# Two transformer blocks in one program: attention banks per head pair, paired expert products, and six buffers for one weight stream

## The chip, the cores and the metric

The kernel runs on one core of one Trainium2 chip. The metric is the time of one execution on the device, in microseconds (us); below 2167.4 us the kernel has become faster. The engines are TensorE (PE for its matmuls, PEld for its weight loads), VectorE (DVE), ScalarE (ACT), GpSimd (POOL) and SyncE (SP), which issues nearly all transfers. All arithmetic is on float32 values.

## The reference, cut to what matters

The program computes two blocks on 256 tokens of width 1024. The first block has two layers: each is a mixer, a SwiGLU network and a gated embedding. The mixer of layer 0, here "the even mixer", is the attention that the change touches:

```python
zb, zc, zh, q, k, v, qi, ki, wi = split_cols(h @ w_in, EVEN_SPLITS)
y_a = zb * causal_dwconv(zc * zh, conv_w)
q = apply_rope(rmsnorm(heads(q), q_norm_g), cos_a, sin_a)   # 8 heads of 64
k = apply_rope(rmsnorm(heads(k), k_norm_g), cos_a, sin_a)
qi, ki = partial_rope(qi, ...), partial_rope(layernorm(ki, ...), ...)
y_b = dsa_attention(q, k, v, qi, ki, wi)   # top-k keys chosen by qi, ki, wi
return concat([y_a, y_b]) @ w_out
```

Layer 1's mixer ("the odd mixer") is a gated delta rule with chunks of 64 tokens. The second block has two layers on the tokens and, in layer 0, on 256 context tokens too. Each takes its shifts, scales and gates from one vector, then mixes, then runs 16 experts, each of which picks 32 tokens of each stream:

```python
sh1, sc1, g1, sh2, sc2, g2 = split(silu(c) @ ada_w[i] + ada_b[i], 6)    # the "ada" product
...
a = einsum('becd,edf->becf', xs, w_gate);  u = einsum('becd,edf->becf', xs, w_up)
y = einsum('becf,efd->becd', silu(a) * u, w_down)                       # 16 experts of 1024 x 1024
```

## The kernel before, in words

The stages stand one behind another in the profile, in us from the span's start: even mixer 0 to 172, its network 172 to 362, embedding and odd mixer 362 to 660, network 660 to 860, embedding and the second block's first mixer (mix2 of layer 0) 860 to 1124, first expert stage 1124 to 1586, mix2 of layer 1 to 1736, second expert stage to the end.

In the dense stages a weight tile is loaded by SP, split into a high and a low part (line 174 on ACT, line 175 on DVE) and multiplied three times: lines 205 to 207 give features by tokens (lines 236 to 238 tokens by features). The code is written against a tile framework: every tile has a pool with a number of buffers, the framework adds the waits, and a scheduler with costs of its own sets the order of each engine's instructions. Each engine then runs its queue strictly in that order, so an instruction that waits holds all behind it. PSUM has eight banks: four of tag "a", three of "b", one of "f" (line 337).

In the even mixer line 485 transposes rotated queries and keys, line 538 makes the index scores. The attention goes over two blocks of 128 queries (tb) and four pairs of heads (hp). Line 601 is the product of queries and keys, lines 605 to 614 the softmax on DVE and ACT, line 617 transposes the probabilities, line 619 copies them, line 621 multiplies them with the values. The PSUM bank of line 621's result is held over all four pairs. Products that do not depend on it (lines 236 to 238 of the convolution branch) are ordered between.

The ada product is a generator (line 1082 on): 96 steps, each one load of 512 KB (line 1096) and four matmuls (line 1111); sixteen steps end in an addition (line 1116) and four transposes (line 1119). The stages before draw on it for steps to fill with, at a priority that lets the scheduler put them where PE would wait. Its tile "adaw" has `nbuf` = 3 buffers.

In the first expert stage both streams of 32 tokens share the stationary side, so 64 columns of PE are used by a gate product (line 1670, PSUM partitions 0 to 63) and the other 64 by an up product (line 1671, partitions 64 to 127). Per expert there are 16 of each, one SiLU and one product of 64x512 for each half n (lines 1681, 1682), transposes of that result (line 1691, eight of 64 rows), a copy (line 1693), 16 down products (line 1702), and every fourth expert gathers the tokens of the next four (line 1631) and scatters the results of four (line 1722). Its weights come as 12 tiles of 1 MB, issued by SP in the order in which the code asks for them (line 1593), into a ring of 24 buffers. An issue waits until its buffer is free and until the transfer eight issues earlier has landed.

## Time and profile before

| | us |
|---|---|
| median of three runs | 2167.4 (2166.94 to 2171.16) |
| profiled execution, its own time | 2173.54 |
| span of the profile | 2171.8 |
| first expert stage | 1124 to 1586 |
| even mixer | 0 to 172 |

The profile is that of one execution. Times of the rows are in us from the start of the span. A 512-column matmul of the expert stages stands in the trace as two records, as do the others on float32 values; a row "x4" is four records without another line between them. The number in brackets is idle time of the engine before the row, and behind the arrow is what ended it. The granted clock (PEclk) is the share of TensorE's full 2.4 GHz.

### The profile page before, as it was taken

How to read it: one execution, taken by the hardware profiler on the slowest of the kernel's cores; microseconds unless marked ns; L12 is line 12 of the kernel's file. 1: busy time of each engine (PE TensorE's matmuls, PEld its weight loads, DVE VectorE, ACT ScalarE, POOL GpSimd, SP SyncE). 2: the span in 40 equal slices, each digit the busy share in tenths (PEclk: the TensorE clock that was granted, in tenths of full speed). 3: DMA queues.
4: the chain of work that ended last, by engine and by line, in shares of the span. 5: the costliest groups of instructions: out<-in, count | busy, mean ns of one | idle time of the engine just before them, and what ended most of it. 6: DMA issues, size and time to landing. Idle time of an engine off the chain costs nothing.

```text
span 2171.8 us, 30574 instructions
## 1 busy us (share of the span) xinstructions
PE 1964.3 (90%) x12300; PEld 1240.6 (57%) x12300; DVE 930.0 (43%) x1969; ACT 669.8 (31%) x1310; POOL 84.2 (4%) x95
## 2 busy tenths in 40 slices
PE   7999999898989999999989999999989788777776
PEld 5687888677867888677753434343357523121211
DVE  7765555785655555754442221322166611010101
ACT  5454444663534444745320000000055300000000
POOL 0100000122010000210000000000000000000000
PEclk9999999999999999999989999999999899998998
DMA  6646676843347676731559999999964699999998
GB/s 237 218 138 232 218 233 199 268 146 108 128 135 233 221 240 205 249 122 57 205 230 415 420 420 420 420 420 418 379 240 175 252 407 420 421 420 420 420 421 341
DMA packets 209086, 611.83 MB, mean 282 GB/s; under 512 B 14736, under 2 KB 117424, under 8 KB 159792
## 3 DMA queue, kind: packets, MB, share of 16 engines
q1 hardware_dynamic: 202320, 603.08, 72.9%
q10 hardware_dynamic: 6624, 6.79, 1.1%
q8 instruction: 97, 1.59, 0.3%
q14 instruction: 45, 0.37, 0.0%
HBM read 608.78 MB, written 1.05 MB: 281 GB/s over the span
## 4 chain that ended last, share of the span: by engine, by line
PE 68%; DMA 20%; DVE 7%; issue 2%; ACT 2%; POOL 1%; SPq 0%; DVEq 0%; ACTq 0%; POOLq 0%
DMA w<-in_w_up_dram 11%; PE ps_a L1671 7%; DMA w<-in_w_down_dram 6%; PE ps_a L206 6%; PE ps_a L205 6%; PE ps_a L207 6%; PE ps_b L1702 5%; PE ps_a L1670 4%; PE ps_b L238 4%; PE ps_b L236 4%; PE ps_b L237 4%; PE ps_f L1111 2%; PE ps_b L1631 2%; DMA adaw<-in_ada_w_dram 2%; DVE wl L175 1%
## 5 line engine op out<-in xcount | busy, mean ns | idle before, releaser
L175 DVE TENSOR_TENSOR wl<-w,wh 128x512 fp32r<-128x512 f32 x540 | 369.7, 694 | 278.1 <-ACT wh L174 275.8
L174 ACT CAST wh<-w 128x512 fp32r<-128x512 f32 x540 | 331.1, 620 | 362.3 <-PE ps_a L207 164.7
L1670 PE MATMUL ps_a<-w,XS 128*64 128x512 f32 x512 | 233.2, 599 | 0.0
L1671 PE MATMUL ps_a<-w,XS 128*64 128x512 f32 x512 | 228.0, 595 | 0.0
L236 PE MATMUL ps_b<-xTh,wh 128*128 128x256 f32 x704 | 200.8, 285 | 0.5 <-ACT wh L174 0.5
L238 PE MATMUL ps_b<-xTh,wl 128*128 128x256 f32 x704 | 199.7, 284 | 1.7 <-DVE wl L175 1.7
L237 PE MATMUL ps_b<-xTl,wh 128*128 128x256 f32 x704 | 198.6, 282 | 0.0
L1742 PE MATMUL ps_b<-w,XS 128*32 128x512 f32 x1024 | 159.2, 633 | 43.5 <-DMA w<-in_w_up_dram 33.4
L236 PEld LDWEIGHTS ps_b<-xTh,wh 128*128 128x128 f32 x704 | 133.1, 189 | 10.0 <-ACT wh L174 8.4
L238 PEld LDWEIGHTS ps_b<-xTh,wl 128*128 128x128 f32 x704 | 134.8, 192 | 6.2 <-DVE wl L175 3.1
L1702 PE MATMUL ps_b<-w,hTe 128*64 128x512 f32 x512 | 138.4, 595 | 0.0
L237 PEld LDWEIGHTS ps_b<-xTl,wh 128*128 128x128 f32 x704 | 133.8, 190 | 2.2 <-issue 1.6
L205 PE MATMUL ps_a<-wh,xTh 128*128 128x512 f32 (+1 forms) x336 | 128.4, 386 | 3.7 <-ACT wh L174 1.9
L206 PE MATMUL ps_a<-wl,xTh 128*128 128x512 f32 (+1 forms) x336 | 129.9, 387 | 0.8 <-DVE wl L175 0.7
L207 PE MATMUL ps_a<-wh,xTl 128*128 128x512 f32 (+1 forms) x336 | 128.9, 384 | 0.0
L1742 PEld LDWEIGHTS ps_b<-w,XS 128*32 128x32 f32 x1024 | 35.6, 112 | 161.8 <-issue 68.8
L1671 PEld LDWEIGHTS ps_a<-w,XS 128*64 128x64 f32 x512 | 67.2, 137 | 102.0 <-issue 100.4
L1744 ACT ACTIVATE sge<-ps_b 64x512 f32<-64x512 f32 x16 | 9.5, 591 | 368.1 <-PE ps_b L1742 368.1
L1681 ACT ACTIVATE sge<-ps_a 64x512 f32<-64x512 f32 x32 | 18.9, 590 | 296.4 <-PE ps_a L1671 253.3
L1756 PE MATMUL ps_b<-w,hTe 128*32 128x512 f32 x512 | 91.2, 724 | 19.8 <-DMA w<-in_w_down_dram 11.5
L1745 DVE TENSOR_TENSOR sge<-sge,ps_b 64x512 f32<-64x512 f32 x16 | 11.0, 690 | 201.1 <-ACT sge L1744 201.1
L1709 DVE TENSOR_TENSOR Y<-ps_b,G 32x512 f32<-32x512 f32 x64 | 44.0, 687 | 104.0 <-PE ps_b L1702 102.8
(534 smaller groups left out, 3231.8 us busy)
## 6 DMA issues: line engine op xcount, KB each, us to landing
w<-in_w_gate_dram SPq DMA_DIRECT2D x128, 1024.0 KB, 19.9
w<-in_w_up_dram SPq DMA_DIRECT2D x128, 1024.0 KB, 19.8
w<-in_w_down_dram SPq DMA_DIRECT2D x128, 1024.0 KB, 19.8
adaw<-in_ada_w_dram SPq DMA_DIRECT2D x96, 512.0 KB, 6.0
w<-in_ffn_w_gate_dram SPq DMA_DIRECT2D x22, 1024.0 KB, 5.2
w<-in_ffn_w_up_dram SPq DMA_DIRECT2D x22, 1024.0 KB, 5.3
w<-in_ffn_w_down_dram SPq DMA_DIRECT2D x22, 1024.0 KB, 5.0
w<-in_od_w_in_dram SPq DMA_DIRECT2D x16, 1024.0 KB, 5.2
```

The lines of the kernel that those rows point to most:

```text
L174: nc.scalar.copy(h, raw)
L175: nc.vector.tensor_tensor(l, raw, h.bitcast(F32), op=ALU.subtract)
L205: mm(out, ah, bh, start=start, stop=False)
L206: mm(out, ah, bl, start=False, stop=False)
L207: mm(out, al, bh, start=False, stop=stop)
L236: mm(o, h[:, s], xT[0][:, k], start=(k == 0 and b % 2 == 0), stop=False, skip_group_check=True)
L237: mm(o, h[:, s], xT[1][:, k], start=False, stop=False, skip_group_check=True)
L238: self.last = mm(o, l[:, s], xT[0][:, k], start=False, stop=(k == nk - 1), skip_group_check=True)
L1670: mm(pg[n][0:64], XS[k][:, e % 4], wt[f"g{k // 2}"][:, k % 2, c], start=(k == 0), stop=(k == 7))
L1671: mm(pg[n][64:128], XS[k][:, e % 4], wt[f"u{k // 2}"][:, k % 2, c], start=(k == 0), stop=(k == 7))
L1702: mm(py[64 * n:64 * n + 64], hv[:, k], wt[f"d{k // 2}"][:, k % 2, n * 512:n * 512 + 512], start=(k == 0), stop=(k == 7))
L1742: mm(pg[32 * q:32 * q + 32], XS[k][:, ex], w[:, k % 2, c], start=(k == 0), stop=(k == 7))
```

## The change

In the even mixer the three projections go to SBUF by a copy as soon as they are complete (k, then v, then q), so their PSUM banks come free; v is projected before q. The index key's transposes are issued behind those of the index queries. Both heads of a pair share one bank for the transposed probabilities and one copy, and line 621's result gets a bank for each pair, which is split to SBUF pair by pair. Several SBUF tiles get more buffers. In the ada product `nbuf` goes from 3 to 6. In the first expert stage the up product is issued first and the gate product directly behind it; the eight transposes of 64 rows become four of 128; the down products take the halves in another order and their tiles are loaded as d0, d2, d1, d3. Three of the next expert's 16 gate and up pairs are now written ahead of the transposes, one behind them.

```diff
-            to_T(ki2, kiT, 1)
-            qi = at.tile([128, 2, 512], F32, tag="tokm", name="qi", bufs=2)
+            qi = at.tile([128, 2, 512], F32, tag="tokm", name="qi", bufs=3)
...
             to_T(qi, qiT, 4)
+            to_T(ki2, kiT, 1)
...
+            def project(c0, name):
+                acc = self.gemm_tok(xT, W, c0, 512)
+                t = at.tile([128, 2, 512], F32, tag="v" if name == "v" else "pj", name=name, bufs=1 if name == "v" else 2)
                 for tb in range(2):
+                    nc.scalar.copy(t[:, tb], acc[tb])
+                return t
...
-            ak = self.gemm_tok(xT, W, 2048, 512)
+            ak = project(2048, "ak")
             norm_rope(1, kT, ak)
-            aq = self.gemm_tok(xT, W, 1536, 512)
+            v = project(2560, "v")
+            aq = project(1536, "aq")
             norm_rope(0, qT, aq)
...
-                        pt = self.ps("b")
+                        if j == 0:
+                            pt = self.ps("b")
                         for kb in range(tb + 1):
-                            nc.tensor.transpose(pt[:, kb * 128:(kb + 1) * 128], pr[:, kb * 128:(kb + 1) * 128], ident)
-                        pT = at.tile([128, 256], F32, tag="pT", name="pT", bufs=2)
-                        nc.scalar.copy(pT[:, :nk], pt[:, :nk])
+                            nc.tensor.transpose(pt[:, j * 256 + kb * 128:j * 256 + (kb + 1) * 128],
+                                                pr[:, kb * 128:(kb + 1) * 128], ident)
+                    nc.scalar.copy(pT[:, :, :nk], pt.rearrange("p (j k) -> p j k", j=2)[:, :, :nk])
+                    po = self.ps("b")
+                    for j in range(2):
+                        h = 2 * hp + j
                         for kb in range(tb + 1):
-                            nc.tensor.matmul(po[64 * j:64 * j + 64, hp * 128:(hp + 1) * 128],
-                                             v[:, kb, h * 64:(h + 1) * 64], pT[:, kb * 128:(kb + 1) * 128],
-                                             start=(kb == 0), stop=(kb == tb))
-                pv = po.rearrange("p (h q) -> p h q", q=128)
-                self.split_to(yT[0][:, 4:8, ts], yT[1][:, 4:8, ts], pv)
+                            nc.tensor.matmul(po[64 * j:64 * j + 64, :128], v[:, kb, h * 64:(h + 1) * 64],
+                                             pT[:, j, kb * 128:(kb + 1) * 128], start=(kb == 0), stop=(kb == tb))
+                    self.split_to(yT[0][:, 4 + hp, ts], yT[1][:, 4 + hp, ts], po[:, :128])
...
-        nbuf = 3
+        nbuf = 6
...
-                        for n in range(2):
-                            c = slice(n * 512, n * 512 + 512)
+                        c = slice(n * 512, n * 512 + 512)
+                        up = mm(pg[n][64:128], XS[k][:, e % 4], wt[f"u{k // 2}"][:, k % 2, c], start=(k == 0), stop=(k == 7))
+                        with self.tc.issue_after(up.ins):
                             mm(pg[n][0:64], XS[k][:, e % 4], wt[f"g{k // 2}"][:, k % 2, c], start=(k == 0), stop=(k == 7))
-                            mm(pg[n][64:128], XS[k][:, e % 4], wt[f"u{k // 2}"][:, k % 2, c], start=(k == 0), stop=(k == 7))
...
-                        gate_up(e + 1, (0,))
+                        gate_up(e + 1, kn[:3])
...
-                    for n in range(2):
-                        for j in range(4):
-                            k = 4 * n + j
-                            nc.tensor.transpose(pt[:, k * 64:(k + 1) * 64], sg[64 * n:64 * n + 64, pair(j)],
-                                                self.ident[64 * n:64 * n + 64, 64 * n:64 * n + 64])
-                        V.tensor_copy(hT[:, n * 256:(n + 1) * 256], pt[:, n * 256:(n + 1) * 256])
+                    for j in range(4):
+                        nc.tensor.transpose(pt[:, j * 128:(j + 1) * 128], sg[:, pair(j)], self.ident)
+                    for j in range(0, 512, 256):
+                        V.tensor_copy(hT[:, j:j + 256], pt[:, j:j + 256])
...
-                    loads(e, [f"d{j}" for j in range(4)])
+                    loads(e, [f"d{j}" for j in (0, 2, 1, 3)])
```

How this moves PE's queue stands in three places. The first is the attention of the even mixer, a pair of heads of the second query block. Before (names as in the lines above: pr are probabilities, kT and qT keys and queries, xTh, wh and wl the convolution branch):

```order
L617 MATMUL ps_b_1109<-const_i_66,pr_1103 128x128 x2
L238 MATMUL ps_a_1386<-xTh_107,wl_1439 128x256
L236 MATMUL ps_a_1387<-xTh_107,wh_1438 128x256
L237 MATMUL ps_a_1387<-xTl_108,wh_1438 128x256
L238 MATMUL ps_a_1387<-xTh_107,wl_1439 128x256
L236 MATMUL ps_a_1387<-xTh_107,wh_1438 128x256
L621 MATMUL ps_b_1094<-pT_1112,v_864 64x128 x2
L617 MATMUL ps_b_1126<-const_i_66,pr_1120 128x128 x2
L601 MATMUL ps_b_1133<-kT_597,qT_596 128x256
L237 MATMUL ps_a_1387<-xTl_108,wh_1438 128x256
L621 MATMUL ps_b_1094<-pT_1129,v_864 64x128 x2
L601 MATMUL ps_b_1134<-kT_597,qT_596 128x256
```

In the changed kernel:

```order
L619 MATMUL ps_b_1108<-const_i_66,pr_1115 128x128 x2
L236 MATMUL ps_a_1542<-xTh_107,wh_1643 128x256
L237 MATMUL ps_a_1542<-xTl_108,wh_1643 128x256
L238 MATMUL ps_a_1542<-xTh_107,wl_1644 128x256
L236 MATMUL ps_a_1542<-xTh_107,wh_1643 128x256
L237 MATMUL ps_a_1542<-xTl_108,wh_1643 128x256
L238 MATMUL ps_a_1542<-xTh_107,wl_1644 128x256
L626 MATMUL ps_b_1124<-pT_1097,v_818 64x128 x4
L602 MATMUL ps_b_1131<-kT_597,qT_596 128x256
L602 MATMUL ps_b_1132<-kT_597,qT_596 128x256
```

Both heads' products with the values (now line 626) stand together, and behind them both of the next pair's products of keys and queries (now line 602).

The second place is PE in mix2 of layer 0, behind the start of its first norm (line 1178, now 1181). Before:

```order
L1111 MATMUL ps_f<-adaw,adastat 32x256 x5
L1178 MATMUL ps_b<-const_i,xn 128x128 x4
L1111 MATMUL ps_f<-adaw,adastat 32x256 x4
L205 MATMUL ps_a<-wh,xTh 128x512
L206 MATMUL ps_a<-wl,xTh 128x512
L1111 MATMUL ps_f<-adaw,adastat 32x256 x3
L207 MATMUL ps_a<-wh,xTl 128x512
L1178 MATMUL ps_b<-const_i,xn 128x128 x4
```

In the changed kernel:

```order
L207 MATMUL ps_a<-wh,xTl 128x512
L1181 MATMUL ps_b<-const_i,xn 128x128 x12
L205 MATMUL ps_a<-wh,xTh 128x512
L206 MATMUL ps_a<-wl,xTh 128x512
L207 MATMUL ps_a<-wh,xTl 128x512
L205 MATMUL ps_a<-wh,xTh 128x512
L1181 MATMUL ps_b<-const_i,xn 128x128 x4
L206 MATMUL ps_a<-wl,xTh 128x512
```

The ada matmuls (line 1111, now 1114) have gone from this stage. 384 of them stand in the program, two records each. At the norm that opens the odd mixer 164 of them stand behind PE before and 192 now; at the norm that follows that mixer 225 and 257; in the changed kernel all 384 stand ahead of the end of the network that ends at 860 us, where before 64 (16 steps) stand behind it.

The third place is PE at the boundary between two experts (sge is the SiLU product that is transposed; ps_a_12685 is the old expert's bank and ps_a_12860 and 12861 the next one's; in the changed kernel 12653, and 12824 and 12825). Before:

```order
L1670 MATMUL ps_a_12685<-w_12815,XS_12683 64x512
L1671 MATMUL ps_a_12685<-w_12817,XS_12683 64x512
L1691 MATMUL ps_b_12871<-const_i_66,sge_12855 128x64 x4
L1670 MATMUL ps_a_12860<-w_12862,XS_12676 64x512
L1670 MATMUL ps_a_12861<-w_12862,XS_12676 64x512
L1691 MATMUL ps_b_12871<-const_i_66,sge_12855 128x64 x4
L1671 MATMUL ps_a_12860<-w_12864,XS_12676 64x512
L1671 MATMUL ps_a_12861<-w_12864,XS_12676 64x512
L1670 MATMUL ps_a_12860<-w_12862,XS_12677 64x512
L1671 MATMUL ps_a_12860<-w_12864,XS_12677 64x512
L1670 MATMUL ps_a_12861<-w_12862,XS_12677 64x512
L1671 MATMUL ps_a_12861<-w_12864,XS_12677 64x512
```

In the changed kernel:

```order
L1674 MATMUL ps_a_12653<-w_12781,XS_12651 64x512
L1676 MATMUL ps_a_12653<-w_12779,XS_12651 64x512
L1695 MATMUL ps_b_12837<-const_i_66,sge_12819 128x128 x4
L1674 MATMUL ps_a_12824<-w_12828,XS_12644 64x512
L1676 MATMUL ps_a_12824<-w_12826,XS_12644 64x512
L1674 MATMUL ps_a_12825<-w_12828,XS_12644 64x512
L1676 MATMUL ps_a_12825<-w_12826,XS_12644 64x512
L1674 MATMUL ps_a_12824<-w_12828,XS_12645 64x512
L1676 MATMUL ps_a_12824<-w_12826,XS_12645 64x512
L1674 MATMUL ps_a_12825<-w_12828,XS_12645 64x512
L1676 MATMUL ps_a_12825<-w_12826,XS_12645 64x512
L1707 MATMUL ps_b_12854<-w_12846,hTe_12836 64x512 x2
```

The gate and up products, which stood two and two with transposes between, alternate one and one. One set of transposes (now line 1695) stands where two did, directly behind the old expert's last pair; four pairs of the next expert follow it, then the 16 down products (now line 1707).

## Rows read from the trace of the kernel before

**Rows 1.** page, part 1: busy us, share of the span, count, by engine
```profile
PE 1964.3 (90%) x12300; PEld 1240.6 (57%) x12300; DVE 930.0 (43%) x1969; ACT 669.8 (31%) x1310; POOL 84.2 (4%) x95
```

**Rows 2.** windows: length, busy of PE, PEld, DVE, ACT, POOL, clock, DMA share, GB/s
```profile
585.00:660.00 75.00, 63.26 (x390) 44.29 (x388) 43.73 (x87) 25.80 (x49) 8.62 (x9) 0.89 0.48 156
860.00:1000.00 140.00, 134.19 (x741) 103.53 (x739) 87.97 (x191) 78.68 (x161) 20.11 (x16) 0.99 0.52 177
1124.00:1586.00 462.00, 451.08 (x1942) 180.53 (x1941) 109.56 (x191) 32.31 (x64) 0.32 (x2) 1.00 0.97 400
1200.00:1500.00 300.00, 292.43 (x1220) 118.99 (x1218) 75.80 (x130) 20.32 (x42) 0.00 (x0) 1.00 1.01 420
1736.00:2172.00 436.00, 335.40 (x1824) 104.10 (x1816) 49.55 (x96) 17.15 (x31) 0.00 (x0) 0.92 0.98 407
```

**Rows 3.** timeline of PE at two expert boundaries: start, length, line, operation [wait]
```profile
1549.13 0.59 PE L1671 MATMUL ps_a<-w,XS 128*64 128x512 f32 x1
...
1549.56 1.88 PE L1671 MATMUL ps_a<-w,XS 128*64 128x512 f32 x4
1551.98 0.69 PE L1691 MATMUL ps_b<-const_i,sge 64*128 64x64 f32 x4 [0.55 <-DVE sge L1682]
1552.60 1.93 PE L1670 MATMUL ps_a<-w,XS 128*64 128x512 f32 x4
...
1574.02 1.88 PE L1671 MATMUL ps_a<-w,XS 128*64 128x512 f32 x4
...
1578.37 7.09 PE L1702 MATMUL ps_b<-w,hTe 128*64 128x512 f32 x32
```

**Rows 4.** timeline of ACT and DVE behind the last gate and up product
```profile
1575.93 0.59 ACT L1681 ACTIVATE sge<-ps_a 64x512 f32<-64x512 f32 x1 [0.27 <-PE ps_a L1671]
...
1576.55 0.69 DVE L1682 TENSOR_TENSOR sge<-sge,ps_a 64x512 f32<-64x512 f32 x1 [0.17 <-ACT sge L1681]
```

**Rows 5.** timeline of SP: the issue of the last four expert tiles
```profile
1541.17 6.35 SPq L1593 DMA_DIRECT2D w<-in_w_down_dram  x4
```

**Rows 6.** DMA issues of 1540 to 1590: count, size, median us to landing
```profile
w<-in_w_down_dram SPq DMA_DIRECT2D x4, 1024.0 KB, 19.1
```

**Rows 7.** instructions on the tile adaw: what they wait for; time to landing
```profile
  DMA adaw<-in_ada_w_dram: 31.0, 23
...
DMA to landing us min/median/max: 3.5/6.0/10.4
```

**Rows 8.** windows of line 1111 alone: PE busy and count of its matmuls
```profile
860.00:1000.00 140.00, 10.61 (x120) 3.59 (x120) 0.99 0.52 177
```

**Rows 9.** waits of PE, 585 to 622: total us, times, longest
```profile
PE ps_f L1111 <- DMA adaw<-in_ada_w_dram: 3.4, 2, 2.9
PE ps_f L1119 <- DVE adarow L1116: 2.6, 1, 2.6
```

**Rows 10.** waits of PE, 622 to 662
```profile
PE ps_f L1111 <- DMA adaw<-in_ada_w_dram: 3.9, 2, 3.0
```

**Rows 11.** waits of PE, 20 to 172
```profile
PE ps_b L485 <- DVE qk L462: 3.7, 2, 2.3
PE ps_b L485 <- DVE ki L513: 1.7, 1, 1.7
```

**Rows 12.** timeline of PE in the first mixer's attention
```profile
118.48 0.28 PE L236 MATMUL ps_a<-xTh,wh 128*128 128x256 f32 x1
118.59 0.28 PE L237 MATMUL ps_a<-xTl,wh 128*128 128x256 f32 x1
118.92 0.44 PE L617 MATMUL ps_b<-const_i,pr 128*128 128x128 f32 x2
119.12 0.37 PE L238 MATMUL ps_a<-xTh,wl 128*128 128x256 f32 x1
...
120.83 0.70 PE L601 MATMUL ps_b<-kT,qT 64*128 64x256 f32 x2
...
125.15 0.38 PE L617 MATMUL ps_b<-const_i,pr 128*128 128x128 f32 x2
```

More of the change, by code (lines that the diff above doesn't have):

```diff
@@ L520, in even_mixer @@
             for tb in range(2):
-                raw = at.tile([128, 512], F32, tag="s2k", name="qraw", bufs=3)
+                raw = at.tile([128, 512], F32, tag="s2k", name="qraw", bufs=4)
                 nc.scalar.copy(raw, acc[tb])
@@ L565, in even_mixer, with norm_rope @@
             kT = at.tile([128, 4, 256], F32, name="kT")
-            def norm_rope(which, dst, acc):
-                xx = at.tile([128, 2, 512], F32, tag="tokm", name="qk", bufs=2)
+            def project(c0, name):
+                acc = self.gemm_tok(xT, W, c0, 512)
+                t = at.tile([128, 2, 512], F32, tag="v" if name == "v" else "pj", name=name, bufs=1 if name == "v" else 2)
                 for tb in range(2):
-                    sq = at.tile([128, 512], F32, tag="s2k", name="qsq", bufs=3)
-                    nc.scalar.activation(sq, acc[tb], AF.Square)
+                    nc.scalar.copy(t[:, tb], acc[tb])
+                return t
+            def norm_rope(which, dst, t):
+                xx = at.tile([128, 2, 512], F32, tag="tokm", name="qk", bufs=3)
+                for tb in range(2):
+                    sq = at.tile([128, 512], F32, tag="s2k", name="qsq", bufs=4)
+                    nc.scalar.activation(sq, t[:, tb], AF.Square)
                     ss = self.small(8)
@@ L581, in norm_rope @@
                 to_T(xx, dst, 4)
-            ak = self.gemm_tok(xT, W, 2048, 512)
+            ak = project(2048, "ak")
             norm_rope(1, kT, ak)
-            aq = self.gemm_tok(xT, W, 1536, 512)
+            v = project(2560, "v")
+            aq = project(1536, "aq")
             norm_rope(0, qT, aq)
-            v = at.tile([128, 2, 512], F32, name="v")
-            acc = self.gemm_tok(xT, W, 2560, 512)
-            for tb in range(2):
-                nc.scalar.copy(v[:, tb], acc[tb])
             yT = self.xt_tiles(KB, "yT", at)
@@ L595, in even_mixer @@
                 ts = slice(tb * 128, tb * 128 + 128)
-                po = self.ps("b")
                 for hp in range(4):
@@ L601, in even_mixer @@
                         nc.tensor.matmul(pp[j][:, :nk], qT[q, hp, ts], kT[q, hp, :nk], start=True, stop=True)
+                    pT = at.tile([128, 2, 256], F32, tag="pT", name="pT", bufs=3)
                     for j in range(2):
-                        h = 2 * hp + j
-                        lg = at.tile([128, 256], F32, tag="lg", name="lg", bufs=2)
+                        lg = at.tile([128, 256], F32, tag="lg", name="lg", bufs=4)
                         nc.vector.scalar_tensor_tensor(lg[:, :nk], pp[j][:, :nk], 0.125, bias[tb],
@@ L608, in even_mixer @@
                         nc.vector.tensor_reduce(nm, lg[:, :nk], axis=AX.X, op=ALU.max, negate=True)
-                        pr = at.tile([128, 256], F32, tag="pr", name="pr", bufs=2)
+                        pr = at.tile([128, 256], F32, tag="pr", name="pr", bufs=4)
                         sm = self.small(1)
@@ L632, in even_mixer @@
             acc = self.gemm_feat(xT, W, 1024, 512)
-            ycv = at.tile([128, 4, 256], F32, tag="tokm", name="ycv", bufs=2)
+            ycv = at.tile([128, 4, 256], F32, tag="pj", name="ycv", bufs=2)
             for b in range(4):
@@ L1710, in moe @@
                     if e < 15:
-                        gate_up(e + 1, range(2, KB))
+                        gate_up(e + 1, kn[4:])
                     if ex == 3:
```

32 lines of the change are left out of this document (16 added, 16 removed).

## Prediction

> **What bounds the kernel now.** I read the page's busy shares first, then the windows by stage, then the waits and timelines of the three stages that the diff touches. PE is busy for 1964 of 2172 us [rows 1], so what shortens PE's queue shortens the span, except where transfers set the pace. The windows show where: in the first expert stage the DMA engines are as full as PE, 1.01 and 420 GB/s over its inner 300 us while PE is busy for 292 of them [rows 2]. A tile of 1 MB (1.0486 million bytes) at 420 GB/s takes 2.50 us, so twelve tiles of an expert take 30.0 us. The reader is to see that two limits stand nearly level there, and that only one is touched by the change. In the second expert stage the transfers alone bind (PE 335 of 436 us, DMA 0.98) [rows 2]; nothing is edited there, and an earlier start of it should pass through to the end one for one, since the transfers that precede it start when the first expert stage gives its buffers back.
>
> **First expert stage, what PE saves.** Between two experts that gather nothing the unpaired record group recurs after 1574.02 - 1549.56 = 24.46 us [rows 3]. Records of one column half follow each other every 0.43 us (1549.13 to 1549.56), whether or not the other half works beside them. A matmul is two records, so a pair of matmuls, one in each half, takes 0.86 us, and so does a single one. Of the 24 pairs of an expert, 22 run paired: 18.9 us. The boundary takes the rest: two up products alone (1549.56), a wait of 0.55 us, a first set of transposes (1551.98 to 1552.60, 0.62 us), two gate products alone (1552.60, 1.86 us), a second set [rows 3]: 5.5 us. In the changed order all 24 pairs are adjacent: 20.6 us. One set of four transposes: I take 0.62 us, the price of four smaller ones; twice that is the upper bound. They stand right behind the old expert's last pair and now need both halves of the product, so PE waits for ACT and DVE. That added wait runs from the end of the last up product, 1575.90, over 0.59 us of ACT to the end of the DVE product at 1576.55 + 0.69 = 1577.24, and with the 0.05 us seen from DVE to PE it is 1.4 us [rows 4]. Queued behind it are four pairs of the next expert, which nothing else waits for; these 3.4 us cover the copy of the transposed result. Sum 20.6 + 0.6 + 1.4 + about 0.2 for the changes of shape = 22.8, that is 1.6 us less per expert and 26 us over sixteen.
>
> **What of it reaches the end.** The transfers do not get faster. The last four tiles are issued until 1547.5 [rows 5] and land 19.1 us later [rows 6], so the last one lands at about 1566.3. PE finishes the down products at 1578.37 + 7.09 = 1585.46 [rows 3], 19.2 us later. It has been running behind its tiles, and saving 26 us makes it catch up. It then waits for the last tile, which holds rows that three of the eight pairs of down matmuls use: 2.6 us. So the stage ends at about 1568.9 in place of 1585.5, 16.6 us earlier. I take 16. If PE saves 0.6 us per expert (transposes at twice the price and a second exposed copy) 9 us stay; more than 17 can't be had without a faster transfer. Issues are in SP's queue in order; each prefetch tile's buffer is given free by the same events as before (weight splits and the output projection of the mixer ahead), so I see nothing late there.
>
> **Ada steps.** Three more buffers move the issue of each load (512 KB) three steps ahead on SP and 1.5 MB into the time up to the first mixer's end. PE's matmul and load queues wait for adaw 31.0 us in 23 cases, a load taking 6.0 us to land [rows 7]; some cases are counted in both queues. Two places show it on PE alone: 3.4 us and a further 2.6 us behind the ada sum at the odd mixer's end, and 3.9 us behind it [rows 9, 10]. With six tiles in hand I expect two thirds of these 9.9 us to go (6.5), and 2 us elsewhere. What is late next at the odd mixer's end is the delta rule's own chain. The second part is that no step is left behind 860 us. There 120 records took 10.6 us of PE [rows 8], 0.71 us a step, and that stage is dense (134 of 140 us [rows 2]): 16 steps, 11.3 us. They are not gone: 28 matmuls more stand ahead of the odd mixer's norm, others in the network behind it. Where PE waits for a norm they are free, in a dense stretch they cost the same. I charge two thirds, 7.5 us. In the odd mixer ACT now issues the load of the index constants and waits there for an ada load to land; the weight splits of the output projection queue behind it, and PE behind these. That costs nothing if the load was issued 6.0 us before, and 6 us if it is issued at that moment; I take 2. Sum 6.5 + 2 + 11.3 - 7.5 - 2 = 10.3, taken as 10, bounds 2 and 18.
>
> **Even mixer.** PE waits 3.7 us for the rotated queries and keys and 1.7 us for the index key [rows 11]. The order puts the value projection and 24 ada matmuls into the first and moves the key's transposes later; I take 4 of these 5.4 us. In the attention each visit to another shape costs: the step to the transposes takes 0.33 us (118.59 to 118.92) where dense matmuls step by 0.11 (118.48 to 118.59) [rows 12], 0.2 us lost. A pair of heads of the second block makes nine such changes before and seven now; over eight pairs that is 16 x 0.2 = 3 us. Against it: from the product of queries and keys to the first transposes 4.3 us pass (120.83 to 125.15) [rows 12], and the last three pairs have only 19 larger matmuls each to fill with, some 4 us for a chain that now contains both heads. I charge 1 us a pair, 3 us. ACT gets four copies of 128x512 at the 0.6 us that its work on one half takes [rows 4], beside PE. Sum +4, bounds -8 and 12.
>
> **Sum.** 16 + 10 + 4 = 30 us off the profiled execution's 2173.5, 2143.5. The median of the runs shown is 6.1 us lower, 2167.4; the same saving gives 2137.
>
> **Rivals.** (1) The ada buffers bring nothing: the moved steps land in dense stretches and ACT's wait takes what the loads give back. For it: most PE waits are not on adaw. Against it: 134 of 140. Time 2167 - 20 = 2147. (2) The expert stage gives little, because transposes and the exposed wait eat the pairing. For it: a wait of 1.4 us replaces one of 0.55. Against it: 3.7 us of unpaired products are plainly there. With 4 us in place of 16: 2149. (3) PE's clock. In the second expert stage, where PE waits for transfers, the granted clock is 0.92; in the first, where it does not, 1.00 [rows 2]. The change makes PE wait in the first as well once it has caught up, about its last five experts. At 0.92 each of these 22.8 us grows by 2, 10 in all, leaving 6 of the 16: 2147. A PE that slows stops waiting, so it can't run away.
>
> The Trainium skill, TensorE: Matmul & The Clock Gate, section "HAM oscillation — how this bites in real kernels", says that a matmul loop whose bursts are shorter than the waits for its weights starts every burst at the half clock. By that rule each of the last bursts would run at 1.2 GHz and rival (3) would be the forecast; the trace agrees only in part, since the second expert stage keeps 0.92 while it waits, not a half.
>
> (4) Slower: the attention's stalls in the even mixer. Its mechanism: three banks of tag "b" now serve two score tiles, one transposed tile and one result for each pair, one more than there are, so a pair can't start before the last is read out, and the 4.3 us chain is exposed whole for each of eight pairs: -34 in place of +4, with the other parts +26, a time of 2167 + 8 = 2175. It decides from 3.3 us more stall a pair. Against it: the products of keys and queries stand behind the last pair's products with the values, with up to 33 convolution matmuls between, 3.7 us.
>
> **Chances.** The forecast 0.60, its own range 2125 to 2146; rival (1) 0.13, (2) 0.10, (3) 0.07, (4) 0.10. About 0.2%, 4 us, is what a measurement of this kernel can tell. Faster: the forecast and nearly all of (1) to (3), 0.87; same 0.05, from a weaker form of (4); slower 0.08. The range for eight in ten: low end with ada at 18 and the even mixer at 10, 2167 - 44 = 2123; high end 2156, past (1) to (3) and half of two of them together.
>
> **What would show it.** Right: in the expert stage the up and gate records start together throughout, an idle of 1.4 us ahead of line 1695, waits of PE on transfers in the last experts, and the last down product within 4 us of the last tile's landing. No line 1114 behind 860 us, less than 4 us of waits on adaw in the odd mixer. In the even mixer fewer waits on line 462, and idle ahead of the last transposes. Wrong: line 1707 ending more than 8 us after the last landing, a granted clock under 0.97 in that stage, ACT idle ahead of the output projection's splits in the odd mixer, or the even mixer ending later than 172 us.

## The result, and the profile after

The changed kernel takes 2141.27 us (median of four runs, 2139.88 to 2142.13) against 2168.31 for the kernel before on the same chip (2166.94 to 2171.16): a ratio of 0.9871, interval [0.9858, 0.9884], or 27 us off. It was run once more on another chip, beside the experiments: 2139.15 against 2167.49, 0.9865 [0.9845, 0.9885]. The forecast was 30 us off and 2137.

PE's busy time falls from 1964.3 us [rows 1] to 1893.1:

```profile
PE 1893.1 (88%) x12236; PEld 1197.9 (56%) x12236; DVE 925.1 (43%) x1975; ACT 670.7 (31%) x1312; POOL 84.8 (4%) x95
```

Windows of the changed kernel, columns as in [rows 2]. The first is the first expert stage, the second a part of its inside, the last the second expert stage:

```profile
1102.00:1561.00 459.00, 415.53 (x1896) 154.38 (x1894) 115.20 (x206) 36.54 (x76) 1.44 (x4) 0.99 0.99 408
1200.00:1450.00 250.00, 229.43 (x1043) 85.72 (x1040) 65.81 (x114) 16.71 (x34) 0.00 (x0) 1.00 1.01 420
1705.00:2140.00 435.00, 327.50 (x1816) 97.44 (x1804) 49.00 (x95) 16.69 (x30) 0.00 (x0) 0.95 0.99 408
```

The transfers of the first expert stage still run at 420 GB/s, but PE is now busy for 229 of 250 us where it was for 292 of 300 [rows 2]: the stage has gone over to its transfers. It does so on the way: PE's first wait for an up tile ends at 1374 us, in the eleventh of the sixteen experts. The second expert stage is as long as before.

Where the time went, by the same events in both traces:

| from the start of the span to, or from event to event | before | after | difference |
|---|---|---|---|
| start to first gate or up product of the first expert stage | 1124.6 | 1102.8 | -21.9 |
| that product to the end of the stage's last down product | 460.8 | 445.1 | -15.7 |
| last down product to the end of the scatter | 8.0 | 12.7 | +4.7 |
| scatter to the end of the program | 578.3 | 579.1 | +0.8 |

The profiled execution of before (2173.54) was 5 us above the median of 2168.31. Five profiles of kernels with the early stages as before reach the stage's first product at 1116.3 to 1124.6, 1120.7 in the mean, and five with the early stages as changed at 1099.7 to 1103.2, 1101.8 in the mean. The first row is thus 18.9 rather than 21.9, and the rows sum to -29.1, against -27.0 and -28.3 by the medians.

**The expert boundary.** PE of the changed kernel between two experts that gather nothing, columns as in [rows 3] (line 1674 is the up, 1676 the gate, 1695 the transpose, 1707 the down product):

```profile
1249.37 0.59 PE L1674 MATMUL ps_a<-w,XS 128*64 128x512 f32 x1
1249.37 0.59 PE L1676 MATMUL ps_a<-w,XS 128*64 128x512 f32 x1
1251.41 0.74 PE L1695 MATMUL ps_b<-const_i,sge 128*128 128x128 f32 x4 [1.44 <-DVE sge L1688]
1252.08 0.64 PE L1674 MATMUL ps_a<-w,XS 128*64 128x512 f32 x1
...
1255.56 7.04 PE L1707 MATMUL ps_b<-w,hTe 128*64 128x512 f32 x32
...
1274.34 0.74 PE L1695 MATMUL ps_b<-const_i,sge 128*128 128x128 f32 x4 [1.44 <-DVE sge L1688]
```

Up and gate start together, the wait ahead of the transposes is 1.44 us, and the four transposes hold PE for 0.67 us (1251.41 to 1252.08). The period is 1274.34 - 1251.41 = 22.93 us. What PE waits for in the whole stage (us in total, times, longest):

```profile
PE ps_b L1695 <- DVE sge L1688: 18.6, 13, 1.4
PE ps_a L1674 <- DMA w<-in_w_up_dram: 13.7, 10, 2.2
PE ps_a L1727 <- DVE Y L1714: 3.9, 1, 3.9
...
PE ps_b L1707 <- DMA w<-in_w_down_dram: 2.7, 2, 1.3
```

The second and fourth lines are the waits for transfers that the forecast spoke of; the third it did not.

**The end of that stage.** PE of the changed kernel:

```profile
1540.79 7.09 PE L1707 MATMUL ps_b<-w,hTe 128*64 128x512 f32 x32 [0.52 <-DVE hTe L1697]
1551.80 1.77 PE L1727 MATMUL ps_a<-Y,Se 128*128 128x512 f32 x2 [3.92 <-DVE Y L1714]
```

PE stands idle for 3.92 us between the last down product and the scatter, and the scatter then starts at half the clock: two records take 1.77 us. Before, it waited 0.88 us there and two records took 1.10:

```profile
1586.34 1.10 PE L1722 MATMUL ps_a<-Y,Se 128*128 128x512 f32 x2 [0.88 <-DVE Y L1709]
```

There the down products are those of [rows 3]. The reader finds the reason in DVE's queue, changed kernel first, then the kernel before:

```profile
1549.82 0.23 DVE L1252 TENSOR_SCALAR qkg<-qkg 128x128 f32<-128x128 f32 x1 [4.96 <-DMA qkg<-in_q_norm_g_dram]
1550.44 0.49 DVE L1445 TENSOR_TENSOR wA<-wr,AB 128x128 f32<-128x128 f32 x2 [0.40 <-DMA wr<-in_w_router_dram]
1550.97 2.85 DVE L1714 TENSOR_TENSOR Y<-ps_b,G 32x512 f32<-32x512 f32 x4
```

```profile
1583.60 0.23 DVE L1249 TENSOR_SCALAR qkg<-qkg 128x128 f32<-128x128 f32 x1 [2.88 <-DMA qkg<-in_q_norm_g_dram]
1584.49 0.49 DVE L1442 TENSOR_TENSOR wA<-wr,AB 128x128 f32<-128x128 f32 x2 [0.67 <-DMA wr<-in_w_router_dram]
1585.51 2.85 DVE L1709 TENSOR_TENSOR Y<-ps_b,G 32x512 f32<-32x512 f32 x4 [0.52 <-PE ps_b L1702]
```

Two small preparations for the next layer's mixer stand ahead of the last expert's scaling (Y), and each waits for a small load. Before, they were done at 1585.0 and Y waited for PE. Now PE was done at 1547.88 and Y waits for them until 1550.97. Their loads are issued from ACT's queue, in the changed kernel at

```profile
1544.49 0.34 ACTq L1250 DMA_DIRECT2D qkg<-in_q_norm_g_dram  x1
```

3.7 us after the down products began; before, 2.0 us after:

```profile
1580.36 0.33 ACTq L1247 DMA_DIRECT2D qkg<-in_q_norm_g_dram  x1
```

ACT waits there for down products of the last expert. At 0.86 us a pair of matmuls, 2.0 us is just behind the second of eight pairs, where the old order has read d0, and 3.7 just behind the fourth, where the new order has read d0 and d2, which alternate. The order of the down tiles is not the whole reason: in e5 below, which keeps the old order, the same load leaves just behind the fourth pair too (5.4 us in, the first pairs there being at half the clock), and in e6, which has the new one, just behind the third (4.5 us in). Which products it waits for, and why that moved, is not shown.

Their landing (KB each, median us) is slower too. From that issue to its landing at 1549.80 the DMA engines are busy for 0.95 of the time and move 292 GB/s; two tiles of 1 MB for the next stage, issued at 1534.46 and 1536.95, stand behind the last expert tiles. Before, the engines moved nothing from 1575.00 to that issue at 1580.36 and were busy for 0.43 of the 3.2 us behind it. Changed kernel first, then before:

```profile
qkg<-in_k_norm_g_dram ACTq DMA_DIRECT2D x1, 64.0 KB, 5.3
```

```profile
qkg<-in_k_norm_g_dram ACTq DMA_DIRECT2D x1, 64.0 KB, 3.2
```

The Trainium skill, DMA: Bandwidth & Descriptors, section "Latency and other measured facts", says that the fixed cost of a transfer is smaller the lighter the memory is loaded; 3.2 against 5.3 us agrees in direction. Whether it is the memory or the tiles ahead in the queues that delays the load, no run here shows.

**Ada steps.** The tile adaw in the changed kernel (first and last start of its matmuls; waits for it; landing):

```profile
L1114 PE MATMUL ps_f<-adaw,adastat x768: 379/379/636, 63.3 to 827.3; 128*32 128x256 f32 x192
...
  DMA adaw<-in_ada_w_dram: 11.8, 8
...
DMA to landing us min/median/max: 3.4/7.0/10.6
```

No step is left behind 827 us, and the waits of 31.0 us [rows 7] are 11.8. In the odd mixer (540 to 660 us) PE's own are

```profile
PE ps_f L1114 <- DMA adaw<-in_ada_w_dram: 5.2, 3, 3.3
```

where they were 3.4 and 3.9, with a further 2.6 behind the sum [rows 9, 10], which is gone.

### The profile page after: what moved, and what is told of

It is laid out like the page before. It is cut to its first block, busy times and chain, and to the rows that moved or that the text cites. A ratio compares the mean times of both kernels' runs of the same rounds, so it can differ in the third digit from the quotient of the medians.

```text
span 2139.7 us, 30448 instructions
## 1 busy us (share of the span) xinstructions
PE 1893.1 (88%) x12236; PEld 1197.9 (56%) x12236; DVE 925.1 (43%) x1975; ACT 670.7 (31%) x1312; POOL 84.8 (4%) x95
## 4 chain that ended last, share of the span: by engine, by line
PE 57%; DMA 28%; DVE 9%; ACT 3%; issue 2%; POOL 1%; SPq 0%; ACTq 0%; DVEq 0%; POOLq 0%
DMA w<-in_w_up_dram 18%; DMA w<-in_w_down_dram 8%; PE ps_a L1674 6%; PE ps_a L206 6%; PE ps_a L205 6%; PE ps_a L207 6%; PE ps_b L236 4%; PE ps_b L238 4%; PE ps_b L237 4%; PE ps_b L1707 3%; PE ps_b L1634 2%; DVE wl L175 2%; PE ps_f L1114 1%; DMA adaw<-in_ada_w_dram 1%; PE ps_b L1354 1%
## 5 line engine op out<-in xcount | busy, mean ns | idle before, releaser
L1674 PE MATMUL ps_a<-w,XS 128*64 128x512 f32 x512 | 231.1, 600 | 13.7 <-DMA w<-in_w_up_dram 13.7
L1707 PE MATMUL ps_b<-w,hTe 128*64 128x512 f32 x512 | 116.4, 596 | 3.2 <-DMA w<-in_w_down_dram 2.7
L1687 ACT ACTIVATE sge<-ps_a 64x512 f32<-64x512 f32 x32 | 18.9, 590 | 295.3 <-PE ps_a L1676 295.1
## 6 DMA issues: line engine op xcount, KB each, us to landing
w<-in_w_gate_dram SPq DMA_DIRECT2D x128, 1024.0 KB, 19.9
w<-in_w_up_dram SPq DMA_DIRECT2D x128, 1024.0 KB, 19.9
w<-in_w_down_dram SPq DMA_DIRECT2D x128, 1024.0 KB, 19.9
```

What stands on the lines that cost most here:

```text
L1674: up = mm(pg[n][64:128], XS[k][:, e % 4], wt[f"u{k // 2}"][:, k % 2, c], start=(k == 0), stop=(k == 7))
L1707: mm(py[64 * n:64 * n + 64], hv[:, j, h], wt[f"d{2 * h + j // 2}"][:, j % 2, n * 512:n * 512 + 512], start=(m == 0), stop=(m == 7))
```

## Experiments

All kernels were timed against the kernel before on the chip that ran them. Its medians were 2168.59 us (e1 to e4), 2167.57 (e5 to e8) and 2167.49 (e9 to e12).

**e1, e2, e3: each part alone.** The kernel before with one part of the diff: the expert stage (e1), `nbuf = 6` (e2), the even mixer (e3).

> The kernel before with the first expert stage of the change alone. Theory: the stage's parts are independent of the others, so the products end about 16 us earlier and the scatter behind them takes about 4.7 us longer, as in the changed kernel: 11 us faster than before, about 2157. Rival: the expert stage gains only because its start was moved (the ring fuller, or the clock otherwise); then it gains clearly less than 8 us here, or, if the longer scatter belongs to the other parts, the full 16.

> The kernel before with six ada buffers in place of three, and nothing else. Theory: the waits of PE and of its weight loads on adaw fall from 31 us to about 12 and no ada step is left behind 860 us; with the steps that move into dense stretches this leaves 6 to 10 us, about 2160. Rival: the steps cost the same wherever they stand and the ada buffers bring nothing: 2168.

> The kernel before with the even mixer of the change alone. The trace of the changed kernel ends the even mixer 11.6 us earlier, with 8 of 384 ada matmuls fewer in it. Theory: 8 to 11 us of that belong to the mixer itself, time about 2158. Rival, as forecast: 4 us, and the rest came from the ada buffers; time about 2164.

| | median us | ratio | interval | us off |
|---|---|---|---|---|
| e1_expert | 2158.32 | 0.9949 | [0.9930, 0.9968] | 11.1 |
| e2_ada | 2160.82 | 0.9967 | [0.9955, 0.9979] | 7.2 |
| e3_even | 2163.31 | 0.9984 | [0.9970, 0.9998] | 3.5 |

(us off is one minus the ratio, times the kernel before.) By the medians alone the three are 10.3, 7.8 and 5.3 us off. The sum is 22, or 23 by the medians, each part uncertain by 2.6 to 4.1 us; the whole change gave 27 and 28. The 4 to 6 us between are about what the three uncertainties together allow. In e1's trace the stage shortens by 15.8 us (15.7 in the whole change), and the scatter ends 4.8 us late: the difference is the 11 measured. So the expert stage's gain does not depend on the other parts, and neither does its loss. In e2 the waits for adaw fall to 8.5 us and no step is left behind 837. The time of e3 is what its rival expected, while its trace reaches the network 11.0 us earlier, as its theory had it; e9 and e10 go into that.

**e4 and e12: the scaling ahead of the preparations.** The changed kernel, with the two DVE products that wait for small loads held behind Y (e12 is the same kernel on the chip of e11):

```diff
-                            V.tensor_tensor(Y[s][32 * ex:32 * ex + 32, n * 512:(n + 1) * 512], py[q], G2[q], op=ALU.mult)
+                            self.lastY = V.tensor_tensor(Y[s][32 * ex:32 * ex + 32, n * 512:(n + 1) * 512], py[q], G2[q], op=ALU.mult)
...
+            with ExitStack() as hold:
+                if i:
+                    hold.enter_context(self.tc.issue_after(self.lastY.ins))
+                V.tensor_scalar(g2[:, 0], g2[:, 0], float(np.float32(128.0 ** -0.5)), None, op0=ALU.mult)
...
+        with ExitStack() as hold:
+            if i:
+                hold.enter_context(self.tc.issue_after(self.lastY.ins))
+            for s in range(2):
+                V.tensor_tensor(wA[:, :, s], wr, AB[s % ns][0][:, :, None].to_broadcast([128, KB, 16]), op=ALU.mult)
```

> The changed kernel, with the two small VectorE operations of the next mixer that need freshly loaded data (the scaling of the query gain and the router weights times the modulation) held behind the last expert's weighting of its result. Theory: at the end of the first expert stage VectorE waits for these small loads, which now meet the last big weight loads, and so weights the result 3.1 us late; that goes, 3 us faster than the changed kernel, about 2138. Rival: the scatter is late because its matmuls run at the half clock; then no change.

> The changed kernel itself, timed on the same chip as the next one. Both theories: 25 to 29 us below the kernel before (2138 to 2143 us).

> The changed kernel with the small preparations for the next layer (the scaled norm weight and the router's weights on VectorE) ordered behind the last expert's scaling of its results, on the same chip as the changed kernel. Theory S (these two products, which wait for small loads, held VectorE's queue for 4.7 us): 3.5 to 5.5 us below the changed kernel, first expert stage ending 8.0 us behind its last down product in place of 12.7. Theory C (the clock or the transfers pace what follows, so the time returns later): within 2 us of the changed kernel.

e4: 2135.33 us, 0.9847 [0.9825, 0.9870]. On one chip, e11, the changed kernel itself: 2139.15 (2138.75 to 2140.38); e12: 2134.75 (2133.95 to 2137.83), 0.9847 [0.9829, 0.9865]. That is 4.4 us below the changed kernel, and no run of the one reaches those of the other. PE and DVE in e12 (its lines 1720 and 1733 are the scaling and the scatter):

```profile
1544.74 2.85 DVE L1720 TENSOR_TENSOR Y<-ps_b,G 32x512 f32<-32x512 f32 x4 [3.07 <-PE ps_b L1713]
```

```profile
1545.58 1.10 PE L1733 MATMUL ps_a<-Y,Se 128*128 128x512 f32 x2 [0.88 <-DVE Y L1720]
```

The scaling waits for PE again, the scatter waits 0.88 us, begins at the full clock and ends 8.0 us behind the last down product, as it did before. The cause of the loss is shown, and of the kernels that do all the work this is the fastest. Not all of it comes out at the end: behind the scatter e12 takes 1.1 us longer than e11 (580.3 for 579.2), and there the clock is at half from 1555.73 to 1565.97, where that of the changed kernel is at full from 1555.60 to 1565.97 (granted clock 0.50 and 1.00).

**e5, e6: halves of the expert edit.** The kernel before with the pairing alone (e5: line 1671 ahead of line 1670 for each half, and three pairs ahead of the transposes) and with the transposes of 128 partitions and the order of the down tiles alone (e6).

```diff
-                        for n in range(2):
-                            c = slice(n * 512, n * 512 + 512)
+                        c = slice(n * 512, n * 512 + 512)
+                        up = mm(pg[n][64:128], XS[k][:, e % 4], wt[f"u{k // 2}"][:, k % 2, c], start=(k == 0), stop=(k == 7))
+                        with self.tc.issue_after(up.ins):
```

```diff
-                    for n in range(2):
-                        for j in range(4):
-                            k = 4 * n + j
-                            nc.tensor.transpose(pt[:, k * 64:(k + 1) * 64], sg[64 * n:64 * n + 64, pair(j)],
...
+                    for j in range(4):
+                        nc.tensor.transpose(pt[:, j * 128:(j + 1) * 128], sg[:, pair(j)], self.ident)
```

> The kernel before with only the order of gate and up products of the change; the eight transposes of 64 rows and the order of the down tiles stay. Theory: an expert then takes PE about 22.9 us (24 pairs 20.6, wait and both sets of transposes 2.1), 1.5 us less than before, which is already more than the transfers allow; the products end about 16 us earlier than before, as with the whole stage changed, and the time falls by 10 to 14 us, to about 2156. Rival: each half of the edit gives its own share; then this one alone gives about half, 6 to 8 us at the products' end.

> The kernel before with only the transposes on 128 partitions and the order of the down tiles that goes with them; gate and up products as before. Theory: PE saves the second set of transposes and the wait (the next expert's two gate products now stand ahead of the transposes), 1.2 us an expert, 19 us in sixteen, again more than the 16.6 that the transfers allow: products end 14 to 17 us earlier, time about 2157. Rival: about half of the gain, as the other half is that of the pairs.

e5: 2157.50, 0.9954 [0.9937, 0.9970]; e6: 2157.28, 0.9952 [0.9934, 0.9970]. In the traces the stage shortens by 14.3 and 13.9 us, against 15.7 for both, so the halves do not add. Behind it the scatter ends 3.4 and 3.0 us late. The transfers stop either half: counted as in the prediction, the last down product ended 19.2 us behind the landing of the last tile before, and ends 4.9 us behind it in e5, 5.2 in e6 and 3.5 with both. PE's waits for up tiles, e6 first, then e5:

```profile
PE ps_a L1671 <- DMA w<-in_w_up_dram: 1.1, 2, 0.6
```

```profile
PE ps_a L1671 <- DMA w<-in_w_up_dram: 6.0, 5, 1.5
```

In e6 PE meets its tiles only in the last expert, in e5 somewhat earlier, and with both there are 13.7 us of waits. On PE itself the halves overlap in part. The period of an expert that gathers nothing was 24.46 us [rows 3], and is 23.31 in e5, 22.89 in e6 and 22.93 with both: with one set of transposes in place of two there are no lone products between two sets, which is what the pairing removes too. The longest of four periods, in which PE gathers and scatters, is 42.2 before, 37.5 in e5, 41.4 in e6 and 37.1 with both. Four experts that wait for no tile (in e5 the shortest period of each kind) take 120.5 us before, 112.3 in e5, 115.1 in e6 and 110.7 in the changed kernel. That is 33, 21 and 39 us less over sixteen experts: each alone is more than the 16.6 that the transfers leave by the prediction's count. A run of either half with fewer transfers, which would show it directly, was not made.

**e7, e8: fewer transfers.** In both, the last quarter of each down matrix is not loaded (another quarter is used in its place), in e7 in the changed kernel and in e8 in the kernel before: 11 MB per expert where there were 12.

```diff
-                    loads(e, [f"d{j}" for j in (0, 2, 1, 3)])
+                    loads(e, [f"d{j}" for j in (0, 2, 1)])
+                    wts[e]["d3"] = wts[e]["d1"]
```

> The changed kernel in which each expert of the first expert stage loads 11 tiles in place of 12 (the last quarter of the down matrix is replaced by the third, so that part of the computation is changed). Theory: the transfers set the pace of that stage; with a twelfth less of them the 16 us in which PE waits for tiles there go, and the products end 14 to 17 us earlier than in the changed kernel, until PE binds. Rival: PE sets the pace as before, and nothing changes.

> The kernel before with the same twelfth of the loads of the first expert stage left out (the last quarter of the down matrix is replaced by the third). Theory: PE sets the pace there, never waiting for a tile, and the products end within 2 us of where they did. Rival: the transfers already set the pace before; then the stage shortens by up to 36 us.

e7: 2114.56, 0.9755 [0.9732, 0.9779]; e8: 2163.21, 0.9989 [0.9973, 1.0005]. The first expert stage, from its first product to the last down product, is 20.7 us shorter in e7 than in the changed kernel (36.5 shorter than before), and 4.5 shorter in e8 than before. Both are more than was expected (14 to 17, and at most 2). The 4.5 are not explained: PE waited for no tile before either, and the order around the gathers is another one (periods of 30.97 for 29.32). Still, the kernel before was bound by PE and gains little from fewer bytes; the changed one is bound by its transfers, and with fewer of them PE waits for no tile in the whole stage. Over four experts PE needs 22.93 + 22.94 + 27.7 + 35.3 = 108.9 us in e7, against 24.46 + 24.46 + 29.3 + 42.2 = 120.5 before: 2.9 us an expert, of which 8.5 of the 11.6 come from the two periods in which tokens are gathered and results scattered. In the changed kernel's own order they take 110.7, as above, 2.4 us an expert less than before. e7 also shows the small loads at the end of the stage at a worse place, in DVE's queue ahead of a SiLU product:

```profile
1512.08 0.23 DVE L1252 TENSOR_SCALAR qkg<-qkg 128x128 f32<-128x128 f32 x1 [6.43 <-DMA qkg<-in_q_norm_g_dram]
1516.06 0.49 DVE L1445 TENSOR_TENSOR wA<-wr,AB 128x128 f32<-128x128 f32 x2 [3.75 <-DMA wr<-in_w_router_dram]
1516.47 1.41 DVE L1688 TENSOR_TENSOR sge<-sge,ps_a 64x512 f32<-64x512 f32 x2
```

PE stands idle for 9.25 us until that product is done, so a part of its saving is lost again in the last expert:

```profile
1517.93 1.12 PE L1695 MATMUL ps_b<-const_i,sge 128*128 128x128 f32 x4 [9.25 <-DVE sge L1688]
```

**e9, e10: halves of the even mixer's edit.** The kernel before with the projections alone (e9: copies to SBUF, v ahead of q, the index key's transposes later) and the attention's banks alone (e10).

```diff
-            ak = self.gemm_tok(xT, W, 2048, 512)
+            ak = project(2048, "ak")
...
+            v = project(2560, "v")
+            aq = project(1536, "aq")
```

```diff
-                        pt = self.ps("b")
+                        if j == 0:
+                            pt = self.ps("b")
...
+                    po = self.ps("b")
```

> The kernel before with only the even mixer's projections changed (copied to SBUF as they complete, v ahead of q, index key's transposes behind the index queries'); attention banks as before. In the profile with all of the even mixer changed its network began 11.0 us earlier than in the profile before, though the times differ by 3.5 to 5.3 us only. Theory P (projections carry it): the network's first norm begins 6 to 10 us earlier than 173.5, waits of PE on rotated queries and keys ahead of the attention fall, time 3 to 5 us below before. Theory B (banks per pair carry it, as the prediction's terms 3 us for shape changes less 3 for the exposed chain leave open): at most 3 us earlier, time within 2 us.

> The kernel before with only the attention's banks changed (both heads of a pair transposed into one bank, one copy, a result bank per pair). Theory P: the prediction's terms cancel, shape changes save 3 us and the exposed chain costs 3, so the network's first norm moves by less than 3 us either way and the time by less than 2. Theory B: 5 us or more earlier. The forecast's rival (4), banks run out: later than before, up to 8 us slower.

e9: 2164.52, 0.9987 [0.9975, 0.9998]; e10: 2161.74, 0.9961 [0.9946, 0.9976]. By the medians alone they are 3.0 and 5.8 us off. The network's first norm begins at 169.4 us in e9, 165.1 in e10 and 162.4 in e3, where it was 173.5 (172.6 to 175.0 in five profiles with the even mixer as before). e10 is what theory B expected of it. e9 lies between its two theories, and B holds for it only once put-off work is counted out. Of e9's 4.1 us most is that: ada matmuls ahead of that norm (line 1111, in e9 1113; columns as in [rows 8]), first the kernel before, then e9:

```profile
0.00:173.50 173.50, 6.39 (x82) 2.14 (x82) 0.99 0.59 197
```

```profile
0.00:169.40 169.40, 2.73 (x26) 0.94 (x26) 0.99 0.55 183
```

These 3.7 us of work are still to be done later, so the projections give about 0.4. e10 has the same 82 records ahead of the norm, and its 8.3 us are real there. They come from two lines. The products of queries and keys (line 601, in e10 600) and with the values (line 621, in e10 624) in the attention, by shape (busy us, mean ns of one), first the kernel before, then e10:

```profile
L621 PE MATMUL ps_b<-pT,v 128*64 128x128 f32 x48 | 8.7, 289 | 0.0
L601 PE MATMUL ps_b<-kT,qT 64*128 64x256 f32 x16 | 5.6, 428 | 0.0
L601 PE MATMUL ps_b<-kT,qT 64*128 64x128 f32 x16 | 3.4, 322 | 0.0
```

```profile
L624 PE MATMUL ps_b<-pT,v 128*64 128x128 f32 x48 | 4.4, 289 | 0.1
L600 PE MATMUL ps_b<-kT,qT 64*128 64x256 f32 x16 | 2.8, 428 | 0.0
L600 PE MATMUL ps_b<-kT,qT 64*128 64x128 f32 x16 | 2.0, 322 | 0.0
```

Count and mean duration are the same, the busy time is halved: 17.7 us become 9.2. The records now lie on top of each other. In the timeline of e10 both heads' products take the time of one head's:

```profile
129.35 0.67 PE L624 MATMUL ps_b<-pT,v 128*64 128x128 f32 x8
129.95 0.70 PE L600 MATMUL ps_b<-kT,qT 64*128 64x256 f32 x4
```

Before, four records of the one took 0.65 us and two of the other 0.70:

```profile
127.98 0.65 PE L621 MATMUL ps_b<-pT,v 128*64 128x128 f32 x4
128.56 0.70 PE L601 MATMUL ps_b<-kT,qT 64*128 64x256 f32 x2
```

The two heads of a pair use different halves of PE (64 rows each in line 601, 64 columns each in line 621). In PE's queue before, the two heads' products stood apart, with others between, and each half worked alone; next to each other they work at the same time. The Trainium skill, TensorEngine Tiling (Array Packing), section "Tiling Modes", says that such tiles operate independently, in parallel; the trace agrees, with 0.67 for eight against 0.65 for four.

## Why the prediction was right, and where it was not

**First expert stage, what PE saves.** Right where it was worked out: 22.93 us a period for 22.8, 1.44 us of wait for 1.4, 0.67 us of transposes for 0.62. Mis-sized in sixteen experts times 1.6 = 26, since the period in which PE gathers and scatters saves 5.1 us and not 1.6: the whole is 16 x 2.4 = 39 in the changed kernel's order and 16 x 2.9 = 46 in that of e7. e6 adds that the transposes alone save the 1.6 at the plain boundary (22.89), without the pairing.

**What of it reaches the end.** Right, and it is why the mis-sized 26 did no harm. The transfers bind. The last four tiles are issued from here on,

```profile
1516.99 7.81 SPq L1596 DMA_DIRECT2D w<-in_w_down_dram  x4
```

the last of them at 1524.5. By the median of 19.9 us to landing it is there at about 1544.4, and the last down product ends at 1547.88, 3.5 us later (forecast 2.6, and under 4 as the sign of being right). The stage became 15.7 us shorter; 16 were forecast, 17 the most.

**The step that failed: "I see nothing late there".** It was said of SP's queue and the prefetch tiles, and of these it held. Nothing was said of the small loads of the next layer, which ACT issues only behind down products of the last expert, nor of what stands ahead of Y on DVE. 4.7 us were lost there: 3.0 of idle PE (3.92 for 0.88), the rest the half clock that the scatter then began with. e4 and e12 give them back at that place. The prediction asked what is late next at the odd mixer's end, and did not ask it behind the last down product.

**Ada steps.** Forecast 10, measured 7.2 (interval 4.5 to 9.8). Waits in the odd mixer fell by 4.7 us (from 9.9 to 5.2), not by 6.5, so the sign "less than 4 us" did not come. No step is left behind 860 us, as forecast. The ACT wait charged with 2 us is not in the trace: none of ACT's larger waits there is on an ada load.

**Even mixer.** Forecast +4, and +3.5 by e3's time; its reasons were wrong. The projections were to give 4 of 5.4 us of waits: PE waits 5.3 us for line 462 in place of 3.7 [rows 11], only the 1.7 us for the index key went, and the net is about 0.4. The banks were to come out even, +3 for shape changes and -3 for the exposed chain: PE is busy for 76.4 of the 77 us of e10's attention, so the chain is not exposed, and the halves that work at the same time save 8.5 us. The prediction read that very thing in the expert stage ("a pair of matmuls, one in each half, takes 0.86 us, and so does a single one") and did not apply it to lines 601 and 621. Up to the network's norm the whole mixer is 11.6 us earlier in the changed kernel, of which 1.3 is ada work put off (66 records of line 1114 ahead of it in place of 82; 11.0, 2.6 and 42 in e3). Why e3's time shows 3.5 (interval 0.4 to 6.5) where e10's shows 8.4 (5.2 to 11.7) is not settled: the intervals meet only at 5 to 6, and by the medians the two are 5.3 and 5.8. The way from that norm to the first expert stage takes 943.5 to 951.2 us in the five profiles with these stages as before and 950.1 in e3, so no trace separates what the stages behind give back from the spread of executions.

**Rivals.** (1) ada nothing: e2 speaks against it. (2) the expert stage little: 15.7 us against it, and still only 11 reach the end, for a reason that was not named. (3) the clock: it did fall to half once in the last expert. PE of the changed kernel there:

```profile
1524.45 0.82 PE L1674 MATMUL ps_a<-w,XS 128*64 128x512 f32 x1 [2.19 <-DMA w<-in_w_up_dram]
...
1525.92 1.06 PE L1674 MATMUL ps_a<-w,XS 128*64 128x512 f32 x1
1526.78 1.06 PE L1674 MATMUL ps_a<-w,XS 128*64 128x512 f32 x1
...
1534.44 0.64 PE L1674 MATMUL ps_a<-w,XS 128*64 128x512 f32 x1 [1.20 <-DMA w<-in_w_up_dram]
```

Pairs of records step by 0.86 us in place of 0.43, for some 4 us behind a wait of 2.19; then PE waits for a transfer again at 1534.44, so the slow stretch cost nothing. The stage's mean is 0.99, not 0.92. Behind a wait just as long, one expert earlier, the clock stayed full (granted 1.00 from 1494.4 to 1498.0):

```profile
1494.46 0.64 PE L1674 MATMUL ps_a<-w,XS 128*64 128x512 f32 x1 [2.20 <-DMA w<-in_w_up_dram]
```

So it is in the traces of e1, e4, e11 and e12 too: full behind the first of these two waits, half behind the second. What decides is not shown. The rule of the Trainium skill that the prediction cited (TensorE: Matmul & The Clock Gate, "HAM oscillation — how this bites in real kernels") is on bursts shorter than the waits for their weights. The bursts here are longer: 3.7 us behind the wait of 2.20, and 8.8 behind that of 2.19. So the rule did not call for a half clock in this stage, and the prediction was mistaken to draw that from it; the trace does not test the rule. (4) the banks: e10 is faster, not slower; nothing ran out.

The total was close by luck in part, because two errors met: by the profiles the early stages gave 18.9 us where 14 were forecast (16 by the medians, 27.0 less the 11.0 of the expert stage), and the stage's end took back 4.7. e2 and e3 together show only 10.7 of the early gain, or 13.1 by the medians, so where the excess came from is open.

## What to carry to other kernels

When a change lets an engine finish a stage earlier, read the in-order queues past that stage's end: small loads and preparations for the next stage that were hidden by the slower work can now stand ahead of the last step of it. Matmuls that use only half of PE's rows or columns should be issued next to a partner on the other half; queued one head after the other they cost double, and the busy share does not show it, only records that stand one behind another do. Where two limits lie within a few per cent, several edits to the one may each give nearly the whole gain by themselves, and the next microsecond has to come from the other.

## What was not expected of the hardware

The two halves of PE work side by side at no visible cost even on the attention's small products: eight records of 128x128 in 0.67 us against four in 0.65. A load of 64 KB took 5.3 us to land while the DMA engines were busy for 0.95 of the time, and 3.2 us where they had moved nothing for the 5 us before. After a wait of 2.19 us in the last expert and one of 3.92 us ahead of the scatter, TensorE ran at half its clock; after one of 2.20 us in the expert before, after those of 1.44 us between experts, and after one of 1.20, it did not.
